# mLSTM norm: centred values, and norm, gate and transposes by pairs of heads

## The chip, the cores and the metric

The kernel runs on one core of a Trainium2 chip. The metric is device time in microseconds, the median of several executions. Its engines each take their instructions in order: TensorE (PE in the profile, its weight loads PEld), VectorE (DVE), ScalarE (ACT), GpSimd (POOL) and SyncE (SP), which here only issues DMA transfers.

## The reference

Two encoder layers on 512 positions of width 1024. In each, one input projection feeds three token mixers (attention with 8 heads, a bidirectional mLSTM with 4 heads of 64, a state-space scan with 4 heads); an output projection joins them, then come a layer norm, a mixture of 16 experts and another layer norm. The change touches the mLSTM's values and its norm. Cut to that:

```python
num = einsum(qk, vc) + w_inter * einsum(qc, C)      # both terms are linear in the values v
h   = num / maximum(abs(den), exp(-m_t))            # den doesn't hold v
h   = scan_forward + flip(scan_backward)            # (512, 4, 64)
mu  = mean(h, -1);  var = mean(square(h - mu), -1)  # over the 64 columns of a head
hn  = (h - mu) * rsqrt(var + 1e-5) * norm_g
y   = sigmoid(o) * hn
```

`num` is a weighted sum of value rows, so the mean of a row of `h` over a head's 64 columns is the same weighted sum of the value rows' means. If each value row has mean zero in each head, `mu` is zero.

## The kernel before

Positions are handled as four tiles of 128 rows (`NT`), heads as two pairs `g`. All matmuls read fp32 data; products that need the precision are made of three products of a high and a low part (`mm3`). Eight PSUM banks are dealt out by hand: banks 0 to 2 (`PA`) take projections and the attention's products, banks 3 and 4 (`PM`) the mLSTM, the rest (`PT_`) scores and transposes. SBUF is a queue of 37 slots (`R.get`, `Q.get`, `free`): the slot freed longest ago is given out next.

The mixer stage is made of generators, each of which stops at every `yield`: `projections` (p), `ssd` (d), `mla_in` (i), `mlstm` (m), and the attention's `scores` (s) and `values` (v). The string `SEQ` (L72, 139 letters) says which is asked for its next step. Its attention part begins with the 38th letter and holds 22 m, 40 s and 40 v. This order gives a priority: the framework's planner reorders instructions by its own estimate of when their inputs will be ready, engine by engine, and places the waits. The position of an m step among the others:

| m step | letter | s and v before it |
|---|---|---|
| 8 | 58 | 10, 4 |
| 9 | 60 | 11, 4 |
| 12 | 77 | 17, 12 |
| 15 | 86 | 20, 15 |
| 16 | 91 | 22, 17 |
| 19 | 103 | 26, 22 |
| 21 | 110 | 29, 24 |
| 22 | 115 | 31, 26 |

(letters counted from 0)

`projections` (L993) makes the mLSTM's queries, keys, the attention's inputs, the values and the gate. For the values (L1038 to L1050) `proj_tm` fills one `PA` bank with a tile of 128 x 256, and a ScalarE copy puts it into `mv1`, whose 65th column per head is one, so that the denominators come out of the same matmuls.

`mlstm` (L1066) takes 16 steps in this version. Step 1 transposes the keys. For each pair, one step makes the states, four the weights of the two heads, and two the forward and backward outputs: numerators, `dn`, division, and in the second direction the sum into `hg`, the pair's part of `hm`. That is steps 2 to 8 for the first pair and 9 to 15 for the second. Step 16 (L1178 to L1209) is the norm for all four heads at once, on tiles of 128 x 1024 (16 groups of 64): VectorE sums and scales the means and subtracts them, ScalarE squares, VectorE sums the squares, takes the inverse root by `rsqrt_` (L426: 11 instructions on 128 x 16), scales and gates by `tho`; then for each pair four TensorE transposes into a `PM` bank, and `finish_heads` (L911) writes the high part (ScalarE) and the low part (VectorE) for the output projection. The last six m letters find the generator at its end.

Beside it each `scores` step takes VectorE for a row maximum and its scaling (`mx`), ScalarE for the exponential, VectorE for the reciprocal of the sum (`sums`) and, for six of the heads, GpSimd (L1338) for the scaling; each `values` step transposes probabilities on TensorE and copies them back. After the stage comes the output projection, whose weights SyncE loads as slots come free.

Of the kernel before, what the change touches and what calls it, by code (L numbers as in the profile page):

```python
# [13 lines left out]
AF = mybir.ActivationFunctionType  # L14
OP = mybir.AluOpType
AX = mybir.AxisListType
# [4 lines left out]
NT = S // 128  # L21
# [67 lines left out]
WPIN = ''  # L89
NU = 7  # L90
WOG = (0, 2)
MG = (16, 16)
PTV = range(8)
GSEQ = 'gzgzgzgzzz'
PHS = (512, 512, 512, 512)
# [91 lines left out]
class Buf:  # L187
# [4 lines left out]
    def free(self):  # L192
        assert self.live
        self.live = False
        self.pool.put(self)
# [17 lines left out]
def tile_trunk(ctx: ExitStack, tc: tile.TileContext, ins, out, dbg=None, depth=DEPTH):  # L213
# [22 lines left out]
    V, A, G, T = Pinned(nc.vector, "V"), Pinned(nc.scalar, "A"), nc.gpsimd, Pinned(nc.tensor, "T")  # L236
# [13 lines left out]
    Q, R = View(pool, F32R), View(pool, F32)  # L250
# [6 lines left out]
    def small(shape, dt=F32, tag="s", bufs=1):  # L257
        return sm.tile(shape, dt, name=nm(tag), tag=tag, bufs=bufs)
# [11 lines left out]
    def tap(name, ap):  # L270
        if dbg is not None and name in dbg:
            nc.sync.dma_start(dbg[name], ap)
# [83 lines left out]
    ident = const.tile([128, 128], F32, name="ident")  # L356
# [202 lines left out]
    for l in range(depth):  # L559
# [431 lines left out]
        mq, mk, mvb, tho, cqb, ckb = [], [], [], [], [], []  # L991

        def projections():  # L993
            for dst in (mq, mk):
# [3 lines left out]
                for g in range(2):  # L998
                    p = proj_fm(w, g * 128, 128)
# [41 lines left out]
            mvb.append(R.get(1040))  # L1041
            mv1 = mvb[0].v("p (i h c) -> p i h c", i=NT, h=4)
            V.memset(mv1[:, :, :, 64:65], 1.0)
            for i in range(NT):
                p = proj_tm(w, i)
                A.activation(mv1[:, i, :, 0:64], p.v("p (h c) -> p h c", h=4), AF.Copy)
                p.free()
                if i % 2:
                    yield
            free(*w)  # L1050
            r = win_next()
# [14 lines left out]
        def mlstm():  # L1066
# [16 lines left out]
            for g in range(2):  # L1083
# [57 lines left out]
                for d in range(2):  # L1141
# [33 lines left out]
                        V.tensor_add(hg, hg, tv)  # L1175
                        free(tb, cb)
                    yield
            free(mq, mk, rows, mvb)  # L1178
            hv = hb_.v("p (a c) -> p a c", c=64)
            mu = small([128, 16], tag="mu")  # L1180
            V.tensor_reduce(mu, hv, axis=AX.X, op=OP.add)
            V.tensor_scalar(mu, mu, 1.0 / 64, None, op0=OP.mult)
            for e, a, b in ((V, 0, MG[0]), (G, MG[0], 16)):
                if b > a:
                    e.tensor_tensor(hv[:, a:b], hv[:, a:b], mu[:, a:b, None].to_broadcast([128, b - a, 64]), op=OP.subtract)
            sq = R.get(1024)
            A.activation(sq.ap, hb_.ap, AF.Square)
            va = small([128, 16], tag="va")
            V.tensor_reduce(va, sq.v("p (a c) -> p a c", c=64), axis=AX.X, op=OP.add)
            sq.free()  # L1190
            V.tensor_scalar(va, va, 1.0 / 64, 1e-5, op0=OP.mult, op1=OP.add)
            rv = rsqrt_(va, 16)
            for e, a, b in ((V, 0, MG[1]), (G, MG[1], 16)):
                if b > a:
                    e.tensor_tensor(hv[:, a:b], hv[:, a:b], rv[:, a:b, None].to_broadcast([128, b - a, 64]), op=OP.mult)
            for i2 in range(2):
                hh = hb_.ap[:, i2 * 512:(i2 + 1) * 512]
                V.scalar_tensor_tensor(hh, tho[i2].ap, 1.0, hh, op0=OP.add, op1=OP.mult)
            free(tho)
            tap("mlstm%d" % l, hb_.ap)  # L1200
            for g in range(2):
                p = PM.get()
                for i in range(NT):
                    T.transpose(p[:, i * 128:(i + 1) * 128],
                                hm[:, i, 2 * g:2 * g + 2, :].rearrange("p h c -> p (h c)"), ident)
                finish_heads(4 + g, p.ap, pth[:, 3 + g, P0 + 6:P0 + 7])
                p.free()
            hb_.free()
            yield  # L1209

# [1019 lines left out]
```

## Time and profile before

| | us |
|---|---|
| median of three runs | 1066.05 |
| lowest, highest | 1061.36, 1069.10 |
| profiled execution | 1070.26 |
| its span, first to last instruction | 1067.8 |

The profile is of one execution. Times in it count from the start of the span. A busy TensorE is not TensorE at its peak: matmuls are pipelined and their ends are modelled, so weight loads are shown beside them. Tiles are named by what the program calls them, without numbers: `s` is any SBUF slot, `b` any PSUM bank, `xt` the transposed input or heads, `mx`, `sums`, `dn`, `mu`, `va`, `rq_y`, `rq_t` small tiles. Nearly all compute instructions are recorded under one helper line, L230, so they are told apart by tile and shape. A releaser is what ended an idle time.

### The profile page before, as it was taken

What the parts mean: (1) busy time and instruction counts of PE and PEld (TensorE: products, weight loads), DVE (VectorE), ACT (ScalarE), POOL (GpSimd) and SP (SyncE); (2) the same over time, 40 slices, a digit from 0 to 9 for tenths busy, and PEclk for the clock granted to TensorE, in tenths of its full rate; (3) what the DMA queues carried; (4) which work ended last, traced back from release to release, by engine and by line L of the source; (5) the groups of instructions that cost most, each with busy time, mean ns of one, the idle gap of its engine ahead of it and who ended that gap; (6) DMA issues with size and microseconds to landing.
All of it is one profiled execution on the core that took longest, in us unless ns stands there. A gap on an engine that the chain in (4) does not pass through costs nothing. (4 is left out here: it accounts for less than half of the span.)

```text
span 1067.8 us, 15553 instructions
## 1 busy us (share of the span) xinstructions
PE 996.5 (93%) x5310; PEld 739.2 (69%) x5310; DVE 836.0 (78%) x1832; ACT 644.6 (60%) x1182; POOL 267.2 (25%) x232
## 2 busy tenths in 40 slices
PE   6999999988998999999999999999799989999995
PEld 6876788555687666666598768876466876666653
DVE  8995557787749799999969955577876498999996
ACT  5565646555524588888646564466464347778874
POOL 1000002223003255565100000022220123556652
PEclk9999989998999899999999998999999989999998
DMA  7211100132656889996532120011347477999933
GB/s 305 69 45 45 40 21 21 35 126 99 234 198 218 282 288 345 335 324 213 204 139 70 40 69 1 21 40 41 118 138 246 168 275 264 311 339 337 308 94 155
DMA packets 51795, 176.76 MB, mean 166 GB/s; under 512 B 8169, under 2 KB 8681, under 8 KB 51712
## 3 DMA queue, kind: packets, MB, share of 16 engines
q1 hardware_dynamic: 45216, 160.42, 42.2%
q0 software_dynamic: 6496, 15.31, 6.0%
q8 instruction: 42, 0.69, 0.3%
q14 instruction: 41, 0.34, 0.1%
HBM read 159.61 MB, written 23.59 MB: 172 GB/s over the span
## 5 line engine op out<-in xcount | busy, mean ns | idle before, releaser
L230 PE MATMUL b<-xt,s 128*128 128x512 f32 (+3 forms) x1484 | 327.1, 367 | 13.8 <-ACT s L230 8.6
L230 PE MATMUL b<-s,s 128*128 128x512 f32 (+7 forms) x1308 | 324.7, 404 | 14.0 <-ACT s L230 7.1
L230 PEld LDWEIGHTS b<-xt,s 128*128 128x128 f32 (+2 forms) x1484 | 234.0, 183 | 80.3 <-issue 11.5
L230 DVE TENSOR_TENSOR s<-s,s 128x1024 fp32r<-128x1024 f32 (+8 forms) x254 | 247.6, 1000 | 50.5 <-ACT s L230 41.7
L230 PEld LDWEIGHTS b<-s,s 128*128 128x128 f32 (+3 forms) x1308 | 185.0, 173 | 99.7 <-DVE s L230 22.6
L230 ACT ACTIVATE s<-b 128x512 f32<-128x512 f32 (+8 forms) x282 | 135.0, 496 | 191.2 <-PE b L230 182.3
L230 ACT ACTIVATE s<-s 128x1024 fp32r<-128x1024 f32 (+5 forms) x219 | 191.6, 910 | 85.1 <-DVE s L230 31.8
L230 PE MATMUL b<-s,xt 128*128 128x256 f32 (+2 forms) x944 | 209.1, 362 | 0.4 <-POOL s L1523 0.4
L230 PEld LDWEIGHTS b<-s,xt 128*128 128x128 f32 (+1 forms) x944 | 150.6, 192 | 34.7 <-issue 4.8
L230 DVE TENSOR_TENSOR xt<-s,xt 128x1024 fp32r<-128x1024 f32 (+1 forms) x106 | 118.3, 1122 | 13.8 <-ACT xt L230 13.7
L230 ACT ACTIVATE xt<-s 128x1024 fp32r<-128x1024 f32 (+1 forms) x107 | 110.4, 1042 | 26.1 <-PE b L230 17.7
L230 PE MATMUL b<-ident,s 128*128 128x128 f32 (+3 forms) x736 | 107.4, 273 | 18.6 <-POOL s L1338 7.7
L230 PEld LDWEIGHTS b<-ident,s 128*128 128x128 f32 (+3 forms) x736 | 81.5, 153 | 53.3 <-ACT s L230 13.9
L1598 POOL DMA_INDIRECT acc<-s,slx x28 | 55.3, 1976 | 99.3 <-ACT s L230 79.4
L230 ACT ACTIVATE s<-b,mx,qsc 128x512 f32<-128x512 f32 x64 | 49.7, 782 | 25.5 <-DVE mx L230 25.1
L1338 POOL TENSOR_SCALAR s<-s,sums 128x512 f32<-128x512 f32 x48 | 37.6, 788 | 105.7 <-DVE sums L230 93.6
L1094 POOL MEMSET s<- 128x780 f32 x4 | 3.0, 756 | 219.9 <-DVE s L230 186.3
L230 DVE TENSOR_REDUCE mx<-b 128x1 f32<-128x512 f32 x64 | 43.2, 686 | 18.3 <-PE b L230 17.9
L1446 POOL DMA_INDIRECT s<-x1d,slx x30 | 40.5, 1351 | 57.4 <-PE b L230 23.0
L230 DVE TENSOR_TENSOR s<-b,s 128x192 fp32r<-128x192 f32 (+3 forms) x92 | 46.9, 524 | 4.6 <-POOL s L1127 2.6
L230 PE MATMUL b<-xt 128*96 128x512 f32 x160 | 48.0, 406 | 1.4 <-DVE xt L230 1.4
L230 ACT ACTIVATE s<-b,slw 96x512 f32<-96x512 f32 (+1 forms) x60 | 39.1, 682 | 14.9 <-PE b L230 8.3
(254 smaller groups left out, 983.9 us busy)
## 6 DMA issues: line engine op xcount, KB each, us to landing
s<-in_w_gu_dram SPq DMA_DIRECT2D x128, 512.0 KB
s<-in_expert_w_down_dram SPq DMA_DIRECT2D x64, 512.0 KB
s<-in_w_inp_dram SPq DMA_DIRECT2D x36, 512.0 KB
s<-in_w_outp_dram SPq DMA_DIRECT2D x16, 512.0 KB
x1d<-s SPq DMA_DIRECT2D x8, 512.0 KB
acc<-s SPq DMA_DIRECT2D x8, 512.0 KB
s<-acc SPq DMA_DIRECT2D x8, 512.0 KB
s<-in_x_t_dram SPq DMA_DIRECT2D x4, 512.0 KB
```

The source lines that it names most:

```text
L230: r = f(*a, **kw)
L1094: G.memset(cb.ap, 0.0)
L1338: (V if hd in NORMV else G).tensor_scalar(P.ap, P.ap, sums, 0.0, op0=OP.mult, op1=OP.add)
L1446: self.ga = G.indirect_dma_start(out=self.xg[:BLK], out_offset=None, in_=x1d[0:128 * n, :], in_offset=bass.IndirectOffsetOnAxis(ap=ix[:BLK ...
L1598: G.indirect_dma_start(out=acc[:, :], out_offset=bass.IndirectOffsetOnAxis(ap=self.ix[:BLK, 0:1], axis=0), in_=yt[:BLK], in_offset=None, b ...
```

## The change

The values are centred when they are evicted: instead of one ScalarE copy, VectorE sums each head's 64 columns out of the PSUM bank into `vm` (128 x 4) and writes the bank less a 64th of that sum into `mv1`, in one instruction over 256 columns. The norm's mean is gone: no sum, no scaling, no subtraction. What is left of the norm moves into the loop over pairs and works on 512 columns (8 groups): ScalarE's square, the sum of squares, gating in two instructions of 256 columns ahead of the inverse root, the inverse root on 128 x 8 and a `yield`; the scaling and a `yield`; the four transposes, `finish_heads` and a `yield`. So `mlstm` has 22 steps: 9 to 11 are the first pair's norm, scaling and transposes, 12 to 18 the second pair's recurrence, 19 to 21 its norm, scaling and transposes. Queries, keys, values and the gates are freed in step 22. `SEQ` stays as it is. `MG`, which could have given part of two norm instructions to GpSimd and gave none, is taken out.

```diff
--- before.py
+++ after.py
@@ -89,7 +89,6 @@
 WPIN = ''
 NU = 7
 WOG = (0, 2)
-MG = (16, 16)
 PTV = range(8)
 GSEQ = 'gzgzgzgzzz'
 PHS = (512, 512, 512, 512)
@@ -1041,11 +1040,17 @@
             mvb.append(R.get(1040))
             mv1 = mvb[0].v("p (i h c) -> p i h c", i=NT, h=4)
             V.memset(mv1[:, :, :, 64:65], 1.0)
+
+            vm = small([128, 4], tag="vm", bufs=2)
             for i in range(NT):
                 p = proj_tm(w, i)
-                A.activation(mv1[:, i, :, 0:64], p.v("p (h c) -> p h c", h=4), AF.Copy)
+                pv = p.v("p (h c) -> p h c", h=4)
+                V.tensor_reduce(vm, pv, axis=AX.X, op=OP.add)
+                V.scalar_tensor_tensor(mv1[:, i, :, 0:64], vm[:, :, None].to_broadcast([128, 4, 64]), -1.0 / 64, pv,
+                                       op0=OP.mult, op1=OP.add)
                 p.free()
                 if i % 2:
+                    vm = small([128, 4], tag="vm", bufs=2)
                     yield
             free(*w)
             r = win_next()
@@ -1175,36 +1180,32 @@
                         V.tensor_add(hg, hg, tv)
                         free(tb, cb)
                     yield
-            free(mq, mk, rows, mvb)
-            hv = hb_.v("p (a c) -> p a c", c=64)
-            mu = small([128, 16], tag="mu")
-            V.tensor_reduce(mu, hv, axis=AX.X, op=OP.add)
-            V.tensor_scalar(mu, mu, 1.0 / 64, None, op0=OP.mult)
-            for e, a, b in ((V, 0, MG[0]), (G, MG[0], 16)):
-                if b > a:
-                    e.tensor_tensor(hv[:, a:b], hv[:, a:b], mu[:, a:b, None].to_broadcast([128, b - a, 64]), op=OP.subtract)
-            sq = R.get(1024)
-            A.activation(sq.ap, hb_.ap, AF.Square)
-            va = small([128, 16], tag="va")
-            V.tensor_reduce(va, sq.v("p (a c) -> p a c", c=64), axis=AX.X, op=OP.add)
-            sq.free()
-            V.tensor_scalar(va, va, 1.0 / 64, 1e-5, op0=OP.mult, op1=OP.add)
-            rv = rsqrt_(va, 16)
-            for e, a, b in ((V, 0, MG[1]), (G, MG[1], 16)):
-                if b > a:
-                    e.tensor_tensor(hv[:, a:b], hv[:, a:b], rv[:, a:b, None].to_broadcast([128, b - a, 64]), op=OP.mult)
-            for i2 in range(2):
-                hh = hb_.ap[:, i2 * 512:(i2 + 1) * 512]
-                V.scalar_tensor_tensor(hh, tho[i2].ap, 1.0, hh, op0=OP.add, op1=OP.mult)
-            free(tho)
-            tap("mlstm%d" % l, hb_.ap)
-            for g in range(2):
+
+                sq = R.get_half()
+                sv = sq.v("p (i e c) -> p i e c", i=NT, e=2)
+                A.activation(sv, hg, AF.Square)
+                va = small([128, 8], tag="va")
+                V.tensor_reduce(va, sq.v("p (a c) -> p a c", c=64), axis=AX.X, op=OP.add)
+                sq.free()
+                for i2 in range(2):
+                    hh = hg[:, 2 * i2:2 * i2 + 2]
+                    V.scalar_tensor_tensor(hh, tho[i2].v("p (a h c) -> p a h c", a=2, h=4)[:, :, 2 * g:2 * g + 2], 1.0, hh,
+                                           op0=OP.add, op1=OP.mult)
+                V.tensor_scalar(va, va, 1.0 / 64, 1e-5, op0=OP.mult, op1=OP.add)
+                rv = rsqrt_(va, 8)
+                yield
+                V.tensor_tensor(hg, hg, rv.rearrange("p (i e) -> p i e", i=NT)[:, :, :, None].to_broadcast([128, NT, 2, 64]),
+                                op=OP.mult)
+                yield
                 p = PM.get()
                 for i in range(NT):
-                    T.transpose(p[:, i * 128:(i + 1) * 128],
-                                hm[:, i, 2 * g:2 * g + 2, :].rearrange("p h c -> p (h c)"), ident)
+                    T.transpose(p[:, i * 128:(i + 1) * 128], hm[:, i, 2 * g:2 * g + 2, :].rearrange("p h c -> p (h c)"),
+                                ident)
                 finish_heads(4 + g, p.ap, pth[:, 3 + g, P0 + 6:P0 + 7])
                 p.free()
+                yield
+            free(mq, mk, rows, mvb, tho)
+            tap("mlstm%d" % l, hb_.ap)
             hb_.free()
             yield
```

## Rows read from the trace of the kernel before

**Rows 1.** Page, part 1: busy us, share of the span, instructions by engine.

```profile
PE 996.5 (93%) x5310; PEld 739.2 (69%) x5310; DVE 836.0 (78%) x1832; ACT 644.6 (60%) x1182; POOL 267.2 (25%) x232
```

**Rows 2.** Stretches: length, then busy us (instructions) by engine, granted clock, DMA share, GB/s.

```profile
core 0: us, PE busy (x) PEld busy (x) DVE busy (x) ACT busy (x) POOL busy (x), PEclk, DMA share, GB/s
128.00:148.00 20.00, 20.00 (x142) 18.92 (x140) 11.38 (x44) 7.75 (x24) 0.76 (x1) 0.83 0.06 20
170.00:290.00 120.00, 110.29 (x545) 73.13 (x545) 93.34 (x231) 71.67 (x160) 28.59 (x34) 0.96 0.31 102
...
697.00:817.00 120.00, 108.76 (x540) 71.88 (x540) 92.11 (x229) 70.59 (x159) 28.54 (x34) 0.97 0.31 102
...
199.00:215.00 16.00, 15.04 (x74) 8.64 (x72) 12.41 (x30) 10.47 (x30) 5.43 (x8) 1.00 0.14 40
...
231.00:248.50 17.50, 11.43 (x38) 5.43 (x37) 14.83 (x34) 8.67 (x15) 5.32 (x5) 0.77 0.18 62
...
727.00:743.00 16.00, 14.68 (x71) 8.32 (x67) 12.17 (x29) 10.64 (x31) 5.68 (x8) 1.00 0.15 46
...
758.50:776.00 17.50, 11.39 (x39) 5.43 (x37) 15.02 (x34) 8.49 (x15) 5.34 (x5) 0.82 0.17 60
...
243.00:246.50 3.50, 3.03 (x6) 0.70 (x6) 3.29 (x8) 1.21 (x3) 0.45 (x1) 0.50 0.00 0
```

**Rows 3.** In order of time, VectorE: start, length, instruction; the first layer's norm.

```profile
231.23 1.22 DVE L230 TENSOR_REDUCE mu<-s 128x16 f32<-128x1024 f32 x1
...
233.76 1.21 DVE L230 TENSOR_TENSOR s<-s,mu 128x1024 f32<-128x1024 f32 x1
...
237.91 1.21 DVE L230 TENSOR_REDUCE va<-s 128x16 f32<-128x1024 f32 x1
...
239.04 0.20 DVE L230 TENSOR_SCALAR mx<-mx,qsc 128x1 f32<-128x1 f32 x1
...
243.92 0.17 DVE L230 TENSOR_TENSOR rq_t<-rq_t,rq_h 128x16 f32<-128x16 f32 x1
...
245.60 1.29 DVE L230 SCALAR_TENSOR_TENSOR s<-s,s 128x512 f32<-128x512 f32 x2
```

**Rows 4.** In order of time, TensorE and its weight loads, [idle before <- releaser].

```profile
230.40 0.60 PE L230 MATMUL b<-ident,s 128*128 128x128 f32 x4
...
242.84 1.36 PE L230 MATMUL b<-ident,s 128*128 128x128 f32 x4 [2.17 <-POOL s L1338]
...
246.56 1.57 PEld L230 LDWEIGHTS b<-ident,s 128*128 128x128 f32 x8 [1.61 <-DVE s L230]
246.56 1.97 PE L230 MATMUL b<-ident,s 128*128 128x128 f32 x8
```

**Rows 5.** In order of time, ScalarE and VectorE, the first layer's value projection.

```profile
129.81 0.39 ACT L230 ACTIVATE s<-b 128x256 f32<-128x256 f32 x1 [0.51 <-PE b L230]
...
132.64 0.38 ACT L230 ACTIVATE s<-b 128x256 f32<-128x256 f32 x1 [2.45 <-PE b L230]
134.32 0.16 DVE L230 TENSOR_SCALAR rms<-b 128x4 f32<-128x4 f32 x1 [2.54 <-PE b L230]
```

**Rows 6.** Groups by form: instructions, busy us, mean ns, idle before; the whole span.

```profile
L230 DVE TENSOR_REDUCE mx<-b 128x1 f32<-128x512 f32 x64 | 43.2, 686 | 18.3 <-PE b L230 17.9
...
L230 DVE TENSOR_TENSOR s<-s,b 96x256 f32<-96x256 f32 x32 | 13.0, 407 | 0.0
...
L230 DVE TENSOR_TENSOR s<-s,s 128x512 f32<-128x512 f32 x23 | 15.7, 688 | 3.6 <-ACT s L230 3.5
...
L230 ACT ACTIVATE s<-s 128x512 f32<-128x512 f32 x16 | 10.1, 634 | 17.8 <-DVE s L230 17.7
...
L230 DVE TENSOR_TENSOR s<-s,s 128x256 f32<-128x256 f32 x12 | 4.9, 422 | 1.3 <-ACT s L230 1.3
...
L230 DVE TENSOR_REDUCE slw<-b 96x1 f32<-96x3 f32 x32 | 4.8, 151 | 3.4 <-PE b L230 3.3
```

**Rows 7.** In order of time, VectorE: an inverse root's step, 8 columns.

```profile
165.37 0.17 DVE L230 TENSOR_TENSOR rq_t<-rq_y 128x8 f32<-128x8 f32 x1
```

## Prediction

> **What bounds the kernel now.** The page's first part says that TensorE is busy for 93% of the span [rows 1], so a change pays where TensorE goes short of work. The chain that ended last doesn't help: it holds only the last tens of microseconds, in the second layer's closing norm, far behind the mLSTM. So I went to the table of stretches, first by tens of microseconds over both mixer stages, then by stages [rows 2]. In the stretch of the value projection (128 to 148) TensorE is busy throughout and VectorE 11.4 of 20 us. In the attention stage, where the mLSTM runs beside the softmax, TensorE is busy 110.3 and 108.8 of 120 us in the two layers, and VectorE 93.3 and 92.1, or 78%. More than half of TensorE's idle time in each layer lies in one stretch of 17.5 us: 231 to 248.5 and 758.5 to 776. Idle there is 17.5 - 11.43 = 6.07 and 17.5 - 11.39 = 6.11 us, and the granted clock is 0.77 and 0.82, while in the 16 us from 199 and from 727 idle is 0.96 and 1.32 us at full clock.
>
> VectorE in order of time [rows 3] tells what this stretch is: the norm of all four heads. The sum for the mean begins it at 231.23 and the gating, two instructions from 245.60, ends it at about 246.9. Between them stand the subtraction, the sum of squares, eleven small steps of the inverse root (one is shown) and the scaling. The norm's big instructions take 1.2 us each (the scaling has the subtraction's shape), and the softmax's own steps queue behind them: the scaling of a row maximum waits until 239.04, behind the whole sum of squares. TensorE in order of time [rows 4] shows the other end: at 242.84 transposes have waited 2.17 us for probabilities that GpSimd scales with a VectorE reciprocal, and at 246.56 the eight transposes of the normed heads have waited 1.61 us for VectorE itself. Those eight take 1.97 us, where four took 0.60 at 230.40: 0.77 us lost per layer to the granted clock, which is 0.50 from 243 to 246.5 [rows 2], its lower level of 1.2 GHz, after idle times of over 2 us.
>
> How large the hole is can be read in two ways. By busy time it is idle beyond the usual rate: 6.07 - 0.96 x 17.5/16 = 5.0 and 6.11 - 1.32 x 17.5/16 = 4.7, with 0.77 of clock twice 11.2 us. By weight loads it is larger: the hole holds 37 in each layer, and the 16 us from 199 and 727 hold 72 and 67, so that work fits into 37/4.5 = 8.2 and 37/4.19 = 8.8 us, and 9.3 + 8.7 = 18.0 us are lost. I take the middle, 14.6, since the loads in the neighbouring stretches belong partly to small mLSTM matmuls, which are quicker to issue than the hole's. The Trainium skill (Perfetto Trace Analysis, Identifying the Most-Contended Engine) says that matmul busy time is a bad measure because matmuls are pipelined, and that the busy share of weight loads is a good one. The rows differ in that direction: weight loads are busy 5.43 of 17.5 us in the hole, matmuls 11.4; by the rule alone the hole would count with 18.0 us and the sum below would end 3.4 us lower.
>
> **The change part by part.** *Evictions.* Eight (four per layer) leave ScalarE, 0.38 us each [rows 5], for two VectorE instructions from PSUM. A sum over 256 columns lies between 0.151 us at 3 columns and 0.686 at 512 [rows 6]; on the line between them it is 0.42. The second, 256 columns in and out, is near the 0.407 of the addition from PSUM: 0.42. So VectorE gains 8 x 0.84 = 6.7 us, and ScalarE loses 3.0. I cost it at nothing on the path: TensorE works throughout there, VectorE has over 8 of 20 us free even with 3.4 more, and a product of the next tile needs another of three banks, while evictions are 2.83 us apart (129.81 and 132.64). What could delay one is VectorE's in-order queue: the instruction at 134.32 waited 2.54 us for TensorE, and the eviction behind it would too; two banks in hand cover about 5.7 us. Without that cover the bound is the whole 6.7 us. Below nothing it isn't: TensorE has no idle time there to win.
>
> *Mean steps removed.* The sum, a small step (as the inverse root's, 0.17) and the subtraction, 1.22 + 0.17 + 1.21 = 2.6 us of VectorE per layer [rows 3].
>
> *Norm by pairs.* With the prices of half the columns [rows 6] the sum of squares is 2 x 0.69 for 1.21, scaling 2 x 0.69 for 1.21, gating 4 x 0.42 for 1.29, and ScalarE squares 512 columns twice, 0.63 each. The small steps don't halve: a step of 16 columns takes 0.17 us and one of 8 columns takes 0.17 as well [rows 3, 7]. An inverse root with the scaling of its sum has twelve, so the second root adds 12 x 0.17 = 2.0 us per layer. VectorE's sum: -2.6 + 0.17 + 0.17 + 0.39 + 2.0 = +0.1 us. So the attention stage's VectorE work stays as it was; only its place changes. The Trainium skill (VectorE: DVE Perf Modes, The TRN2 errata) speaks against this part: each VectorE instruction pays a fixed cost, so many small ones pay it many times. The two rows on the small steps agree; by its 58 cycles at 0.96 GHz, an estimate from that page, twelve steps would add 0.7 us instead of 2.0.
>
> *Where it goes.* The first pair's tail, 0.69 + 0.84 + 0.17 + 1.9 + 0.69 = 4.3 us of VectorE, now stands between the first pair's sum of directions and the second pair's states. The second pair's recurrence moves behind it, its tail into the steps where 26 to 29 of 40 score steps are queued instead of 22. Each pair is cut into three steps, between which the planner has softmax steps to issue. The norm's burst becomes two of 4.3 us, and no norm instruction holds VectorE over 0.7 us. The ends of this gain: if everything TensorE loses in the two stages came back, 120 - 110.3 + 120 - 108.8 + 1.5 of clock = 22.4 us; if nothing did, 0.
>
> *A wait added.* TensorE's in-order queue now meets normed heads twice per layer. Behind them stand score products and transposes, and behind those ScalarE's and VectorE's evictions. Between nothing and the 1.61 us of the present wait, I take 1.6 for the added one, as the planner placed the present one: 3.2 us.
>
> *Buffers.* Queries, keys, values and gates are freed 24 letters of the order string later, at the last of 22 mLSTM steps. The attention's 102 letters take 120 us, so that is about 28 us. SyncE's queued loads for the output projection that take these buffers wait that much longer, and the loads behind them in its queue too. I give it nothing: the projection's bulk follows the stage's end at 290, 43 us after the norm's present end at 247, and DMA is busy 0.31 of the stage [rows 2], so 15 us of cover stay. If they are gone, TensorE idles at 290 by what is missing, at most the 28 us of the delay.
>
> Sum: -14.6 + 3.2 + 0 = -11.4 us. The profiled execution took 1070.3 us (span 1067.8), 4.2 above the median of the three runs; taken from its own time this gives 1058.9, and from the median, which the result will be measured against, 1066.05 - 11.4 = 1054.6. I say **1054.5**.
>
> **Rivals.** (a) *The hole closes*, as above: 1054.5, own range 1044 to 1060. For it: the hole is where the norm is, twice, and VectorE is not full elsewhere.
> (b) *The hole moves.* From 199 to 215 VectorE is already busy 12.4 of 16 us; 4.3 more are 16.7, over the stretch. If VectorE's order, not the burst, starves the softmax, TensorE loses around 205 what it wins around 240, and the planner may put the small steps of both pairs in one piece all the same, so that the change does nothing for the order. Gain 0 to 4 us: 1062 to 1066, with evictions exposed up to 1066 + 6.7 = 1073. Against it: the second pair's recurrence moves out of the same stretch.
> (c) *Two holes*, on the other side. The chain from sum of squares to scaling is serial. If TensorE comes to the first pair's transposes before VectorE has scaled that pair, it stands still as it now does, with the softmax behind: a second idle of 6.1 us and 0.77 of clock per layer, +13.7 us: 1080. It decides once weight loads around 205 and 735 fall from some 70 in 16 us to the hole's rate, 37 in 17.5. Against it: that chain is 4.3 us long, half of what stands there now, and has two breaks in it. The Trainium skill's fixed cost of small instructions (the section named above) works to this side.
>
> **Chances.** (a) 0.62, (b) 0.27, (c) 0.11. A measurement of this kernel can tell about 1%, 10.7 us. Of (a), 0.50 lies beyond that and 0.12 within; (b) lies within; (c) is slower. Faster 0.50, same 0.39, slower 0.11. The range goes from 1066 - 22.4, or 1043.5, to (b)'s upper end, 1073; outside it are most of (c) and a little below.
>
> **What would show it.** The hole's idle time falls from 6.1 us to 1 to 3 per layer, its clock stays near 1.0, and no stretch of 17 us in the attention stage holds fewer than 60 weight loads: (a). VectorE near full and TensorE idle around 200 to 215: (b), or 37 loads there: (c). TensorE idle between 128 and 148: the evictions weren't hidden. VectorE's busy time should grow by 6 to 8 us in all, ScalarE's fall by 2 to 3. I am wrong if VectorE's total, rather than its burst, sets the softmax's pace.

## The result and the profile after

The changed kernel takes 1059.2 us (median of 14 runs, 1054.6 to 1066.1) against 1065.0 for the kernel before beside it: ratio 0.9948, 95% interval 0.9928 to 0.9968, or 5.5 us less. The profiled execution took 1056.9 us with a span of 1055.2. Below, a difference in us is a ratio's distance from 1 times 1065.

The page of the changed kernel, part 1 (busy us, share, instructions), answers [rows 1]:

```profile
PE 986.2 (93%) x5310; PEld 730.0 (69%) x5310; DVE 842.6 (80%) x1874; ACT 643.4 (61%) x1176; POOL 266.5 (25%) x232
```

VectorE gained 6.6 us, ScalarE lost 1.2. The stretches of the changed kernel (columns as in [rows 2]) show where the hole went:

```profile
128.00:148.00 20.00, 19.99 (x164) 18.62 (x162) 16.35 (x57) 7.80 (x25) 0.75 (x1) 1.00 0.09 27
...
190.00:206.00 16.00, 13.44 (x54) 7.68 (x54) 13.37 (x42) 8.72 (x19) 3.31 (x4) 0.89 0.00 1
237.00:253.00 16.00, 12.44 (x52) 8.18 (x52) 12.90 (x45) 7.56 (x16) 2.79 (x4) 0.89 0.40 123
709.00:725.00 16.00, 12.80 (x66) 7.78 (x67) 14.73 (x48) 9.24 (x20) 3.85 (x5) 1.00 0.20 67
758.00:774.00 16.00, 12.89 (x60) 8.22 (x59) 15.04 (x49) 8.34 (x18) 4.11 (x6) 1.00 0.42 140
```

Each layer had one stretch with 6.1 us of idle TensorE; now it has two, at the first pair's tail (190 and 709) and at the second's (237 and 758), with 2.56 + 3.56 and 3.20 + 3.11 us: the idle time of these stretches together is about unchanged (12.2 us before, 12.4 after). They are shallower, though. They hold 52 to 67 weight loads in 16 us where the old one held 37 in 17.5 [rows 2], and the clock is 0.89 and 1.00 instead of 0.77 and 0.82. With the rates of the neighbouring stretches of before (4.5 and 4.19 loads per us) these loads fit into 12.0, 11.6, 16.0 and 14.1 us, so 10.3 us are lost where 18.0 were: 7.7 regained, 0.9 of them in the first layer (9.3 to 8.4) and 6.8 in the second (8.7 to 1.9). By busy time, idle beyond the usual rate is 12.4 - 4.6 = 7.9 us (0.96 and 1.32 us per 16, twice each) against 9.7: 1.8 regained, 3.3 if all 1.5 us of clock came back. The measured 5.5 lies between 3.3 and 7.7.

One wait of the old hole is gone. In the kernel before, the transposes at 242.84 [rows 4] waited for probabilities; GpSimd, then VectorE beside it (start, length, instruction, [idle before <- releaser]):

```profile
240.51 2.27 POOL L1338 TENSOR_SCALAR s<-s,sums 128x512 f32<-128x512 f32 x1 [3.21 <-DVE sums L230]
```

```profile
241.00 1.21 DVE L230 TENSOR_TENSOR s<-s,s 128x1024 fp32r<-128x1024 f32 x1
```

In the prediction I read this wait as one for a VectorE reciprocal. GpSimd had that when it began at 240.51, but this scaling took 2.27 us, and 42 of the 48 scalings of that trace take 0.73 us or less. The second layer's hole has the same (2.28 us at 768.18). During it VectorE ran instructions that read two SBUF tiles; that they draw the scaling out was not tested by itself. In the changed kernel the longest scaling takes 1.23 us.

Why half a norm still stops TensorE: three of the four tails hold one long wait for ScalarE (196.21, 720.84, 246.74). In order of time, first ScalarE, then TensorE, at the first pair of the first layer of the changed kernel:

```profile
194.91 0.63 ACT L229 ACTIVATE s<-s 128x512 f32<-128x512 f32 x1 [2.07 <-DVE s L229]
195.56 0.60 ACT L229 ACTIVATE s<-b 128x512 f32<-128x512 f32 x1
```

```profile
196.21 0.66 PE L229 MATMUL b<-ident,s 128*128 128x128 f32 x4 [1.80 <-ACT s L229]
```

The instruction at 194.91 is the norm's square. It stands at the head of ScalarE's queue for 2.07 us, until VectorE has added the pair's directions; the softmax's eviction behind it empties its bank at 196.16, and the next four transposes, which fill such a bank, begin at 196.21. In the second layer it is the same, with 2.01 and 1.57 us:

```profile
719.54 0.63 ACT L229 ACTIVATE s<-s 128x512 f32<-128x512 f32 x1 [2.01 <-DVE s L229]
```

```profile
720.84 0.66 PE L229 MATMUL b<-ident,s 128*128 128x128 f32 x4 [1.57 <-ACT s L229]
```

At the second pair of the first layer it is VectorE's queue. VectorE, ScalarE, TensorE of the changed kernel:

```profile
242.88 0.69 DVE L229 TENSOR_REDUCE mx<-b 128x1 f32<-128x512 f32 x1 [1.40 <-PE b L229]
...
244.18 0.68 DVE L229 TENSOR_REDUCE va<-s 128x8 f32<-128x512 f32 x1
244.77 0.75 DVE L229 SCALAR_TENSOR_TENSOR s<-s,s 128x256 f32<-128x256 f32 x2
...
245.51 0.21 DVE L229 TENSOR_SCALAR mx<-mx,qsc 128x1 f32<-128x1 f32 x1
...
250.17 0.68 DVE L229 TENSOR_TENSOR s<-s,rq_y 128x512 f32<-128x512 f32 x1
```

```profile
245.81 0.78 ACT L229 ACTIVATE s<-b,mx,qsc 128x512 f32<-128x512 f32 x1 [1.21 <-DVE rq_y L229]
```

```profile
246.74 0.66 PE L229 MATMUL b<-ident,s 128*128 128x128 f32 x4 [1.50 <-ACT s L229]
```

A row maximum begun at 242.88 is scaled only at 245.51: between them stand another row maximum, the norm's sum of squares and its gating. ScalarE's exponential waits for that (the releaser named, rq_y, is the instruction beside the scaling on VectorE), and four transposes wait 1.50 us for ScalarE. The normed heads' own transposes hardly count: from 238 to 256 TensorE's waits for VectorE are 1.1 us in all. The three long waits make 4.9 us; the rest of what TensorE loses in the tails was not followed to its waits.

A mixer stage is measured here from the cumulative sums of the log gates (la) to the router's logits (lg): the first start of a row is the first layer's, the last the second's. The changed kernel (ns fastest/mean/slowest, first to last start):

```profile
L229 PE MATMUL b<-la,tri_u x4: 220/272/276, 51.3 to 579.6; 128*128 128x32 f32 x4
L229 DVE COPY lg<-b x8: 177/178/179, 298.3 to 822.8; 128x20 f32<-128x20 f32 x8
```

A second execution of the kernel before, without the low clock that the first had in its projections [rows 2, from 128]:

```profile
L230 PE MATMUL b<-la,tri_u x4: 209/272/276, 52.3 to 580.9; 128*128 128x32 f32 x4
L230 DVE COPY lg<-b x8: 178/179/179, 299.3 to 829.1; 128x20 f32<-128x20 f32 x8
```

That is 247.0 and 243.2 us after, 247.0 and 248.2 before: nothing less in the first layer, 5.0 us less in the second. (The spans of these two executions differ by 7.9 us, so 2.9 lie outside the stages.) In the first layer the hole was split and not filled.

### The profile page after: what moved, and what is told of

The parts are those of the page before. It is cut to its first block, busy times and chain, and to the rows that moved or that the text cites. A ratio compares the mean times of both kernels' runs of the same rounds, so it can differ in the third digit from the quotient of the medians.

```text
span 1055.2 us, 15594 instructions
## 1 busy us (share of the span) xinstructions
PE 986.2 (93%) x5310; PEld 730.0 (69%) x5310; DVE 842.6 (80%) x1874; ACT 643.4 (61%) x1176; POOL 266.5 (25%) x232
## 5 line engine op out<-in xcount | busy, mean ns | idle before, releaser
L229 ACT ACTIVATE s<-s 128x1024 fp32r<-128x1024 f32 (+4 forms) x221 | 192.0, 904 | 93.1 <-DVE s L229 42.5
L229 ACT ACTIVATE s<-b 128x512 f32<-128x512 f32 (+7 forms) x274 | 132.5, 499 | 169.2 <-PE b L229 160.8
L229 PE MATMUL b<-s,xt 128*128 128x256 f32 (+2 forms) x944 | 202.2, 353 | 1.0 <-DVE s L229 0.5
L229 PEld LDWEIGHTS b<-s,xt 128*128 128x128 f32 (+1 forms) x944 | 145.0, 184 | 35.2 <-issue 4.8
L229 PEld LDWEIGHTS b<-ident,s 128*128 128x128 f32 (+3 forms) x736 | 80.6, 151 | 52.9 <-ACT s L229 14.5
L229 DVE TENSOR_REDUCE mx<-b 128x1 f32<-128x512 f32 x64 | 43.6, 686 | 15.1 <-PE b L229 14.5
```

The source lines that it names most:

```text
L229: r = f(*a, **kw)
```

## Experiments

**The kernel before, profiled again.** Nothing is changed.

> The kernel before, profiled once more. If the clock's fall between 134 and 141 and between 660 and 668 belongs to the order of its instructions, this profile has it again at the same places. If it comes and goes from execution to execution, it is missing or elsewhere here, and the 3.2 us that the two profiles differ by in each projection stage aren't the change's.

Measured: 1065.9 us, span 1063.1. Its stretches:

```profile
128.00:148.00 20.00, 19.89 (x160) 18.06 (x158) 13.30 (x49) 9.36 (x27) 0.76 (x1) 1.00 0.08 27
...
228.00:245.50 17.50, 11.41 (x40) 5.43 (x38) 15.17 (x34) 8.35 (x15) 5.27 (x5) 0.83 0.21 64
757.00:774.50 17.50, 11.29 (x39) 7.21 (x40) 13.28 (x32) 9.50 (x16) 6.02 (x4) 0.80 0.20 70
```

The hole is there again, with 6.1 and 6.2 us of idle; the clock of 0.83 in the projections is not.

**Is the hole worth what I put on it?** The norm taken out of the kernel before; gating and transposes stay:

```diff
-            mu = small([128, 16], tag="mu")
...
-                    e.tensor_tensor(hv[:, a:b], hv[:, a:b], rv[:, a:b, None].to_broadcast([128, b - a, 64]), op=OP.mult)
             for i2 in range(2):
```

> The kernel before without the norm: no mean, no variance, no scaling; gating and transposes stay. It leaves that part of the computation out, to price the hole from above. If the norm's burst is the hole's cause, the hole is gone: by the forecast's reckoning 11 to 18 us faster. If the hole is made by the order of the softmax's own steps at that place, 0 to 5 us faster and idle time of TensorE stays there.

Measured: ratio 0.9872 (0.9831 to 0.9914), 13.6 us less. In the stretch that held the hole in the second execution, 228 to 245.5, TensorE is now busy 16.32 us and not 11.41:

```profile
228.00:245.50 17.50, 16.32 (x74) 9.83 (x72) 12.83 (x29) 11.12 (x22) 6.18 (x6) 1.00 0.19 64
```

So the hole is the norm's. The interval, 9.2 to 18.0 us, holds the 14.6 that I took and leaves open which of the two readings, 11.2 or 18.0, was nearer.

**Evictions alone.** The kernel before with centred evictions on VectorE; the norm keeps its mean steps:

```diff
-                A.activation(mv1[:, i, :, 0:64], p.v("p (h c) -> p h c", h=4), AF.Copy)
...
+                V.tensor_reduce(vm, pv, axis=AX.X, op=OP.add)
+                V.scalar_tensor_tensor(mv1[:, i, :, 0:64], vm[:, :, None].to_broadcast([128, 4, 64]), -1.0 / 64, pv,
+                                       op0=OP.mult, op1=OP.add)
```

> The kernel before, with only the centred evictions of the values on VectorE; the norm of four heads and its mean steps stay as they were (they now take the mean of values whose mean is nearly nothing). VectorE gains 6.7 us, ScalarE loses about 3. Theory 1 (evictions are hidden under TensorE in the projection stage): within 2 us of before, and the 2.6 us by which centring alone was slower come from the changed order behind it. Theory 2 (the evictions cost on the path): 3 to 7 us slower, with idle of TensorE between 128 and 148 above 0.5 us, and the mean steps that the centring alone took away were then worth 0 to 4 us.

Measured: 0.9984 (0.9964 to 1.0005). VectorE's 5 to 6 us more (842.1 us by this run's page, 836.0 and 837.0 by the two of the kernel before) cost nothing that can be measured. TensorE stays busy through the projection stretch:

```profile
128.00:148.00 20.00, 20.00 (x155) 19.08 (x155) 14.34 (x54) 6.54 (x21) 0.76 (x1) 0.91 0.10 27
```

**Centring alone.** The same evictions, and the mean steps go; still one norm for four heads:

```diff
-            mu = small([128, 16], tag="mu")
-            V.tensor_reduce(mu, hv, axis=AX.X, op=OP.add)
...
-                    e.tensor_tensor(hv[:, a:b], hv[:, a:b], mu[:, a:b, None].to_broadcast([128, b - a, 64]), op=OP.subtract)
```

> Centring at the eviction alone: VectorE evicts centred values and the mean's three steps are gone; the norm is still one step for all four heads. If the burst makes the hole (the forecast), a burst of 8.3 us of VectorE that loses 2.6 us closes about a third of it: 2 to 5 us faster. If the change pays by pairs only, no difference. If the evictions weren't hidden, 2 to 6 us slower, with idle time of TensorE between 128 and 148. If moving evictions off ScalarE is what keeps TensorE's clock at 1.0 between 134 and 141 (before: 0.50 there), the profile shows 1.0 there in both layers and some 3 us less in each projection stage.

Measured: 1.0024 (1.0002 to 1.0046), 2.6 us more: a miss. With 2.6 us less of VectorE in each norm the kernel is 4.3 us above the run that kept them (about 1 to 7 by the two intervals). The stretches, then TensorE and GpSimd in order of time:

```profile
230.00:240.00 10.00, 4.21 (x14) 1.95 (x13) 8.79 (x27) 5.58 (x10) 3.61 (x2) 0.78 0.31 105
240.00:250.00 10.00, 8.71 (x24) 5.67 (x25) 2.70 (x4) 2.87 (x5) 3.52 (x3) 0.53 0.17 52
```

```profile
240.58 2.82 PE L230 MATMUL b<-ident,s 128*128 128x128 f32 x12 [3.37 <-POOL s L1337]
```

```profile
237.08 3.44 POOL L1337 TENSOR_SCALAR s<-s,sums 128x512 f32<-128x512 f32 x1 [3.44 <-DVE sums L230]
```

VectorE has work for only 2.70 of the 10 us from 240. TensorE's order now has twelve transposes in one group, and the group waited 3.37 us for probabilities that GpSimd scales; behind it VectorE ran dry, and the clock fell to 0.53. That scaling took 3.44 us where most take 0.69, while VectorE ran the gating and an instruction on 128 x 1024 beside it, and the second layer has the same at 766.22. At 0.69 us it would have ended 2.75 us sooner in each layer, an estimate that covers the 4.3 us. So the length of VectorE's burst does not by itself set the hole. What runs beside GpSimd's scaling and where the planner puts transposes in TensorE's in-order queue are candidates; this run doesn't separate them.

**By pairs alone.** The change without centring: ScalarE evicts, and each pair takes its own mean:

```diff
...
+                V.tensor_reduce(muv, hg, axis=AX.X, op=OP.add)
+                V.tensor_scalar(mu, mu, 1.0 / 64, None, op0=OP.mult)
+                V.tensor_tensor(hg, hg, muv[:, :, :, None].to_broadcast([128, NT, 2, 64]), op=OP.subtract)
                 sq = R.get_half()
```

> Norm, gate and transposes by pairs alone: ScalarE evicts as before, and each pair takes its own mean and subtracts it. If the burst makes the hole, this alone brings most of the change's 5.5 us (4 to 7 us faster), although VectorE has 2.6 us more per layer in the attention stage than the change leaves. If the hole only moves (VectorE's total sets the pace), within 2 us of before. With the hole split, no stretch of 17 us of the attention stage has 6 us of idle TensorE, but two have 2 to 3.

Measured: 0.9969 (0.9947 to 0.9990), 3.3 us less, between what the two theories gave. It holds the same two half-holes, the second of 2.98 us:

```profile
190.00:200.00 10.00, 8.10 (x38) 4.39 (x37) 9.53 (x26) 5.78 (x14) 2.67 (x3) 1.00 0.03 12
...
240.00:250.00 10.00, 7.02 (x32) 4.30 (x33) 9.03 (x30) 5.82 (x12) 3.13 (x4) 1.00 0.20 69
```

Its interval and the change's overlap, so what centring adds to the pairs, 2.2 us, is not established.

**Place without the cut.** The kernel before, the second pair's recurrence and the norm of all four three letters later:

```diff
                         free(tb, cb)
                     yield
+                if g == 0:
+                    for _ in range(3):
+                        yield
```

> The kernel before, its norm of all four heads unchanged, but the second pair's recurrence and so the norm moved three steps of the order string later, to where the change has them. Theory 1 (what the change wins is the norm being cut in two): as before, within 2 us of 1065, with the hole of 5 to 6 us per layer moved some 8 us later. Theory 2 (the place in the string is what wins): 3 to 5 us faster, 1060 to 1062, with the hole's idle at 3 us per layer or less. A third: slower by 2 to 6 us, since the later hole ends closer to the stage's end.

Measured: 1.0048 (1.0027 to 1.0069), 5.1 us more, as the third guess had it; its reason was not tested. The hole is spread over 30 us, 2.74, 2.39 and 1.68 us of idle:

```profile
230.00:240.00 10.00, 7.26 (x35) 5.44 (x35) 8.22 (x22) 1.98 (x4) 4.09 (x2) 0.90 0.52 171
240.00:250.00 10.00, 7.61 (x27) 4.49 (x27) 8.40 (x21) 7.16 (x14) 2.10 (x3) 0.84 0.28 93
250.00:260.00 10.00, 8.32 (x36) 5.53 (x34) 9.51 (x21) 4.89 (x7) 0.70 (x1) 0.92 0.46 157
```

**Cut without the place.** The changed kernel, with the first pair's tail using none of the three letters, so that the second pair begins where it stood:

```diff
                 rv = rsqrt_(va, 8)
-                yield
+                if g:
+                    yield
...
                 p.free()
-                yield
+                if g:
+                    yield
```

> The changed kernel, with the first pair's tail (squares to transposes) in the step of its last direction instead of three steps of its own, so that the second pair's recurrence begins three letters earlier, where it stood before the change; the second pair's tail keeps its steps. Moving the uncut norm three letters later had cost 5.1 us. Theory 1 (the change wins by the cut and loses by the later place): 3 to 6 us below the changed kernel, 1053 to 1056, and faster than both. Theory 2 (with the norm cut, the second pair has to go later, since the first tail and the second recurrence would crowd VectorE in one place): 0 to 4 us above the changed kernel, 1059 to 1063, with VectorE over 9 of 10 us and TensorE idle over 3 in the stretches from 190 to 210.

Measured: 1.0072 (1.0051 to 1.0093), 7.7 us above before and 13 above the change; theory 1 fell, and theory 2 has the direction but not the size. The stretches, then TensorE in order of time:

```profile
190.00:200.00 10.00, 7.54 (x33) 4.04 (x32) 9.50 (x30) 4.61 (x11) 1.74 (x3) 1.00 0.15 53
200.00:210.00 10.00, 6.97 (x35) 3.74 (x34) 7.12 (x22) 5.88 (x15) 1.96 (x3) 1.00 0.16 54
```

```profile
229.29 0.33 PE L229 MATMUL b<-ident,s 128*128 128x128 f32 x1 [2.26 <-POOL s L1342]
...
268.56 1.67 PE L229 MATMUL b<-s,xt 128*128 128x512 f32 x4 [2.55 <-POOL s L409]
```

From 190 to 200 the first pair's tail and the second pair's recurrence meet on VectorE, busy 9.50 of 10 us while TensorE idles 2.46. But the change has 9.04 and 2.57 there, so this crowding doesn't explain the loss. From 200 to 210 TensorE idles 3.03 us where it idles 0.84 in the change, and over both attention stages (165 to 292 and 692 to 822) its waits for GpSimd are 13.3 us here and 3.6 there: the larger part of the 13. Why GpSimd is late here was not tested. The later place alone costs 5.1 us, the cut alone 7.7, and both together save 5.5: neither has a price of its own.

**The breaks in the tail.** The changed kernel, each tail in one step, the two letters left over standing empty behind it:

```diff
                 rv = rsqrt_(va, 8)
-                yield
...
                 p.free()
                 yield
+                yield
+                yield
```

> The changed kernel, with each pair's tail (squares, sum, gating, root, scaling, transposes) in one step of the order string instead of three; the two steps taken out stand empty behind it, so that the next pair begins where it did. Theory 1 (the breaks in the tail let softmax steps in between, and this is part of the gain): 2 to 5 us slower than the changed kernel, 1061 to 1064, with idle of TensorE around 195 and 245 above its 2.6 and 2.9 us in 10. Theory 2 (the planner orders the instructions by their costs and the steps hardly matter): within 1.5 us of the changed kernel, 1058 to 1061.

Measured: 0.9954 (0.9935 to 0.9972), as the change. TensorE's and VectorE's busy time in the two tails of the first layer repeat the change's to 0.1 us:

```profile
190.00:206.00 16.00, 13.45 (x54) 7.60 (x53) 13.38 (x41) 8.78 (x19) 3.29 (x4) 0.89 0.02 7
237.00:253.00 16.00, 12.44 (x51) 7.97 (x50) 12.88 (x45) 7.56 (x16) 2.78 (x4) 0.89 0.40 132
```

The two breaks inside a tail do nothing; the planner deals its small steps out by itself.

**What is left of the norm's price.** The changed kernel without squares, sum, root and scaling:

```diff
-                A.activation(sv, hg, AF.Square)
-                va = small([128, 8], tag="va")
-                V.tensor_reduce(va, sq.v("p (a c) -> p a c", c=64), axis=AX.X, op=OP.add)
...
-                rv = rsqrt_(va, 8)
...
-                V.tensor_tensor(hg, hg, rv.rearrange("p (i e) -> p i e", i=NT)[:, :, :, None].to_broadcast([128, NT, 2, 64]),
-                                op=OP.mult)
```

> The changed kernel without squares, sum, inverse root and scaling; gating, transposes, centred evictions and the three steps of a pair stay. It leaves the norm out of what is computed. Without any norm the kernel before took 13.6 us less. Theory 1 (the change only gets back part of the hole, the rest is still in the two smaller ones): 7 to 10 us below the changed kernel, 1049 to 1052. Theory 2 (the norm is hidden in the changed kernel, and something else that it brought, evictions or later buffers, eats the rest): 0 to 3 us below it, 1056 to 1059.

Measured: 0.9853 (0.9820 to 0.9886), 10.1 us below the change by the ratios (6 to 14 by the two intervals), 8.6 by the medians. The two kernels without a norm are 2 us apart, less than the error of either, so no cost of the rest of the change shows. Of the 13.6 us that the norm took before it still takes about 10.

The mixer stages, measured as above, tell it by layer; the kernel before without its norm, then the changed one without it:

```profile
L230 PE MATMUL b<-la,tri_u x4: 216/272/276, 52.5 to 573.3; 128*128 128x32 f32 x4
L230 DVE COPY lg<-b x8: 178/179/179, 293.1 to 817.2; 128x20 f32<-128x20 f32 x8
```

```profile
L229 PE MATMUL b<-la,tri_u x4: 191/270/276, 52.3 to 574.6; 128*128 128x32 f32 x4
L229 DVE COPY lg<-b x8: 177/178/179, 291.2 to 816.2; 128x20 f32<-128x20 f32 x8
```

They last 240.6 and 243.9 us, and 238.9 and 241.6. Against the stages with a norm (247.0 and 248.2 before, 247.0 and 243.2 after) the norm took 6.4 us in the first layer and 4.3 in the second before, and takes 8.1 and 1.6 now. One execution each: the change hides most of the norm in the second layer and none of it in the first.

**Less VectorE, longer chain.** The changed kernel, the root's three iterations on GpSimd:

```diff
-                rv = rsqrt_(va, 8)
...
+                for _ in range(3):
+                    G.tensor_tensor(t8, rv, rv, op=OP.mult)
+                    G.tensor_tensor(t8, t8, h8, op=OP.mult)
+                    G.tensor_scalar(t8, t8, 1.5, 1.0, op0=OP.add, op1=OP.mult)
+                    G.tensor_tensor(rv, t8, rv, op=OP.mult)
```

> The changed kernel with the three iterations of each pair's inverse root on GpSimd; VectorE loses ten small steps a pair, about 1.7 us a pair and 6.8 us in all, and the chain from sum to scaling gets longer. Theory 1 (the norm's remaining price is VectorE's time in its stretches): 2 to 5 us below the changed kernel, 1054 to 1057. Theory 2 (it is the order: GpSimd's queue also scales the probabilities that TensorE's transposes wait for, and the chain to the normed heads' transposes grows): 0 to 6 us above, with longer waits of TensorE for GpSimd around 195 and 245.

Measured: 1.0023 (1.0008 to 1.0038), 8 us above the change: theory 2, and more than it gave. GpSimd, then TensorE in order of time:

```profile
244.43 0.20 POOL L1198 TENSOR_SCALAR rq_h<-va 128x8 f32<-128x8 f32 x1
...
247.73 0.20 POOL L1203 TENSOR_TENSOR rq_y<-rq_t,rq_y 128x8 f32<-128x8 f32 x1
247.91 1.89 POOL L1347 TENSOR_SCALAR s<-s,sums 128x512 f32<-128x512 f32 x2
```

```profile
249.19 0.47 PE L229 MATMUL b<-ident,s 128*128 128x128 f32 x1 [3.02 <-POOL s L1347]
```

The root holds GpSimd from 244.43 to 247.93, the scaling of the probabilities queues behind it, and TensorE waits 3.02 us for that. VectorE's busy time fell only from 842.6 to 839.8 us by the pages, and not by the 6.8 that were expected, so theory 1 had less to win than it said. What is seen is that the softmax stands behind the norm in another queue.

**The softmax first.** The changed kernel, with priority for the row maximum and its scaling:

```diff
-                    V.tensor_reduce(mx, pS.ap, axis=AX.X, op=OP.max)
-                    V.tensor_scalar(mx, mx, qsc[:, 1, i:i + 1], None, op0=OP.mult)
+                    with tc.high_priority(100):
+                        V.tensor_reduce(mx, pS.ap, axis=AX.X, op=OP.max)
+                        V.tensor_scalar(mx, mx, qsc[:, 1, i:i + 1], None, op0=OP.mult)
```

> The changed kernel with one thing added: the softmax's row maximum and its scaling are given a priority of 100 instructions over the rest in the planner, nothing is computed otherwise. In the changed kernel's trace a row maximum taken at 242.88 is scaled only at 245.51, behind the norm's sum, gating and first small steps; the exponential waits for it and four transposes of TensorE for 1.50 us behind that. Theory 1 (what remains of the norm's price is VectorE's order, norm ahead of softmax): 3 to 7 us below the changed kernel, 1052 to 1056, and the waits of TensorE for ScalarE at 196 and 246 below 0.5 us. Theory 2 (VectorE is full there, so whichever goes first, the other is late): within 2 us of the changed kernel, with the waits moved to other tiles.

Measured: 0.9932 (0.9909 to 0.9955), 1.7 us below the change, within both intervals. VectorE in order of time, the stretches, and a later wait, GpSimd then TensorE:

```profile
240.33 1.29 DVE L229 TENSOR_REDUCE mx<-b 128x1 f32<-128x512 f32 x2 [0.26 <-PE b L229]
241.53 0.33 DVE L229 TENSOR_SCALAR mx<-mx,qsc 128x1 f32<-128x1 f32 x2
```

```profile
240.00:250.00 10.00, 9.70 (x45) 6.35 (x44) 9.59 (x32) 6.99 (x15) 3.21 (x4) 1.00 0.42 120
...
710.00:720.00 10.00, 6.39 (x32) 4.30 (x32) 7.15 (x24) 5.24 (x12) 3.98 (x3) 0.98 0.34 107
```

```profile
716.68 2.59 POOL L1340 TENSOR_SCALAR s<-s,sums 128x512 f32<-128x512 f32 x1 [1.99 <-DVE dn L229]
```

```profile
719.33 0.35 PE L229 MATMUL b<-ident,s 128*128 128x128 f32 x1 [1.94 <-POOL s L1340]
```

At 240 the first two row maxima are scaled at once and TensorE is busy 9.70 of 10 us, where the change has 7.14: the hole closes there, with the norm's work all the same. At 710 of the second layer it idles 3.61 us instead of 2.36; the scaling that it waits for there took 2.59 us on GpSimd and not 0.69. At 196 nothing could change, since the wait there is ScalarE's: in this run too TensorE waits 1.5 us there. So theory 1 holds at the place from which it was read, and theory 2 for the sum.

**Priority in the first layer alone.**

```diff
-                    with tc.high_priority(100):
+                    with tc.high_priority(100 if l == 0 else 0):
```

> The changed kernel with the row maximum's priority in the first layer alone; by the orders of the instructions the first layer is then that of the run with the priority in both layers, the second that of the changed kernel. In that run the first mixer stage had lasted 242.3 us against 247.0 in the changed kernel, the second 246.4 against 243.2. Theory 1 (a stage's time is set by the order of its instructions and comes back with it): 242 to 243 us in the first layer and 243 to 244 in the second, 3 to 5 us below the changed kernel, 1054 to 1056. Theory 2 (the differences between these two runs' stages are scatter between executions): within 2 us of the changed kernel, with stage times that lie anywhere between.

Measured: 0.9946 (0.9925 to 0.9967), as the change. The stretches:

```profile
240.00:250.00 10.00, 9.64 (x44) 6.06 (x43) 9.69 (x29) 6.72 (x14) 3.20 (x4) 1.00 0.32 106
...
710.00:720.00 10.00, 7.79 (x35) 4.54 (x34) 8.85 (x27) 5.39 (x13) 2.45 (x3) 1.00 0.29 104
```

Each layer's order brought its stretches back: 9.64 us at 240 as in the run before, 7.79 at 710 as in the changed kernel (7.64). Its stages lasted 243.8 and 244.2 us, 2.2 less than the change's two, at a clock of 0.91 from 128 to 148 where the change and the run with both priorities had 1.00, but the median did not follow. Span less stages is 570.9 us here and 565.0 in the changed kernel: between these two executions the rest of the program differs by more than the stages do. No version was shown to beat the changed kernel.

## Why the prediction was right in kind and too large

**The hole** was read rightly in the main: it is the norm's, and 13.6 us (9.2 to 18.0) against 14.6 forecast. One wait in it was read wrongly: 2.17 us for GpSimd were a scaling drawn out to 2.27 us, and not VectorE's reciprocal. The 18.0 us that the prediction put down to a rule go by the number of weight loads. The Trainium skill (Perfetto Trace Analysis, Identifying the Most-Contended Engine) names their busy share and not their number. That share is 5.43 us of the hole's 17.5 against 8.64 and 8.32 of 16 beside it [rows 2], from which I estimate 14.5 us, and the 13.6 agree. For the changed kernel it doesn't hold: by the same measure 3.9 us would be left, and about 10 are.

**Evictions, mean steps, buffers** were costed at nothing on the path. For evictions and buffers no cost showed: evictions alone 0.9984 with 1 inside the interval, TensorE busy 19.99 of 20 us there, and at 280 to 290, where late output weights would show, 10.00 of 10. The mean steps got no price of their own: taking them out alone went with 4.3 us more. The new instructions took 0.420 and 0.415 us against 0.42 each, the sum of squares of a pair 0.68 against 0.69. VectorE's total grew by 6.6 (6 to 8), ScalarE's fell by 1.2, less than the 2 to 3 forecast. Most small steps of 8 columns took 0.15 to 0.17 us, so the 2.0 us for twelve more steps stands, and the lower estimate of 0.7 us fell. VectorE's work in the attention stage stayed within 2 us of [rows 2] per layer, as counted. (In `SEQ` itself steps 12 to 22 stand one letter later than in the table of m steps, 78 to 116; the delay of 24 letters is the same.)

**The added wait is the term that was mis-sized.** I replaced a loss of 14.6 us by 3.2, two waits of TensorE for normed heads. What the norm still costs is about 10 us, and it isn't that wait. I took "no norm instruction holds VectorE over 0.7 us" for a short wait of the softmax. But a queue keeps its order: a softmax step waits for all of the norm's steps ahead of it and for what these wait for, 2.0 us of ScalarE for VectorE at the first pairs, 2.6 us from row maximum to scaling at the second, and TensorE behind them 1.5 to 1.8 us each time, 4.9 us in all. The rest of the 10 us is measured by leaving the norm out, but its waits were not traced. Put as a sum: -13.6 for the old norm, about +10 for the new one, and -2 for the rest, which is within its error, give -5.5.

**A tail of 4.3 us** was the sum of busy times. From the sum at 244.18 to the end of the scaling at 250.85 the chain took 6.7 us, since softmax steps stand between its small steps; at the first pair, from 195.57 to 206.58, it took 11.0.

**Rivals.** The change is faster by half a per cent, within the 1% that I named and not beyond it as the likeliest case had it. That it fell into the range says little, since this is 30 us wide (1043.5 to 1073). It lies between (a) and (b): 1059.2 is inside (a)'s own range and 4.7 above its value, while the marks are half of each. By layer, the first stage does what (b) said: it takes no less time (247.0 us both) and has as much idle as before, in two places. The second, 5.0 us shorter, is nearer to (a). The old place closed only in part (idle 3.1 to 3.6 instead of 6.1, where 1 to 3 were to show (a)), the stretch of 17 us from 237 to 254 holds 54 loads (60 were to show it), and a second hole stands at 190 and 709 as (b) said, with VectorE at 9.0 of 10 us from 190 to 200. (c) named this second hole and gave it the old one's depth; it has half of that, idle 2.56 and 3.20 us with 54 and 67 loads in 16 us against 37 in 17.5. That the second pair's recurrence moves away, which I had counted against (b), turned out to be needed: without it the change is slower by 13 us.

**What stays open.** Why the same edit pays in the second layer and not in the first, and what draws GpSimd's scaling out in the old hole, with centring alone and with the priority. Why these orders come out as they do: every edit lets the planner reorder the instructions behind it, so that removing work (centring alone) can cost 4 us, and a priority that adds no work can close one hole and open another. Moving the square behind the softmax's eviction in ScalarE's queue, which the first pairs' waits suggest, was not tried. That a different order could keep both layers' gains is suggested by the two priority runs, not shown.

## What to carry to other kernels

When a block of work that stops the bound engine is cut in half, cost each half as a block again: look what the neighbours' chains (here row maximum, exponential, transposes) will wait for behind it in each in-order queue, not how long one instruction holds an engine. Price a hole by bounds, its idle time and its missing weight loads; the measured price lay between them here, with an interval as wide as the two. Compare by layer before crediting a mechanism: this gain lies in one of two that run the same code. A cut and a shift that come in one change can each be a loss and together a gain, so test them apart before crediting either.

## What the hardware showed unexpectedly

In the same program the granted clock was 0.83 from 128 to 148 in one execution [rows 2] and 1.00 in another, 0.91 in several variants, with TensorE busy for at least 19.89 of the 20 us each time. The first mixer stage took 250.3 us in the one and 247.0 in the other, the second 250.3 and 248.2. A difference of 3 us in one profiled stage is therefore no evidence for a change until the clock's column has been compared.

GpSimd's scaling of 128 x 512 took 0.69 us as a rule, but 2.27 us in the old hole, 3.44 with centring alone and 2.59 with the priority. For 2.0, 2.5 and 1.9 us of these VectorE ran instructions that read two SBUF tiles; beside the 571 scalings of at most 0.75 us in the 14 traces it ran such instructions for 0.08 us on average. No run changes this overlap alone, so that it is the cause is not shown.

GpSimd takes 0.20 us for a step of 8 columns, near VectorE's 0.17, but dependent steps followed each other every 0.28 us there (244.63, 244.91, 245.20), against 0.20 on VectorE (245.91, 246.11, 246.31).
